# Three separate PSUM tiles for SwiGLU's seven products, a third plain block, and four early steps of the second product

## The chip, the core and the metric

The kernel runs on one core of a Trainium2 chip. The metric is the time of one launch on the device, in microseconds (us). Each kernel was run several times; its median is quoted, and one further execution was recorded by the hardware profiler, which is where all rows below come from.

## The reference, cut to what matters

One decoder layer with 1024 tokens of width 1024, all in float32. A token mixer with three branches comes first. The part that the change touches is the second half, SwiGLU with 2816 hidden columns:

```
x = layer_norm(ALPHA * x + (1 + g1) * mixer(...), ln1_g, ln1_b)
u = x * (1 + sc2) + sh2
gate, up = split(u @ ffn_w1, 2)           # (1024x1024) @ (1024x5632)
h = (silu(gate) * up) @ ffn_w2            # (1024x2816) @ (2816x1024)
x = layer_norm(ALPHA * x + (1 + g2) * h, ln2_g, ln2_b)
```

## The kernel before, in words

**Precision.** Every float32 operand is split into two parts, a rounded "high" part and the remainder ("low"). ScalarE (ACT) makes the high part and VectorE (DVE) the low one (`split`, lines 106 to 108). A product is three matmuls: high by high, high by low, low by high. A matmul has 128 weights rows and columns and 512 moving columns and writes 128x512 floats of PSUM, which are one of the two halves of a 128x1024 tile.

**First product.** The 2816 hidden columns are 22 blocks of 128. The first `NPL` blocks are "plain": gate and up are computed by `dense` (line 143) for all 1024 tokens, 2 parts x 8 slices of the contraction x 3 x 2 halves of the tokens = 96 matmuls. The other blocks use a Strassen-Winograd scheme over the four quarters (halves of the contraction by gate and up): seven products (`product`, line 1103) of 4 x 3 = 12 matmuls each, 84 in all, from sums of weights (`sums`: s1, s2, s3, s4 and the plain quarters, made one block ahead) and from sums of activations T1 to T4 (lines 1154 to 1168, made once, into buffers that the plain blocks read too).

In a block the seven products are issued in this order: py with s2 and T2; px with w11; pz with s1 and T1; py with s3 and T3, added to the first; px with w12, added; pz with s4, added; py with w22 and T4, added. Between them ACT copies py and px out (`u2_`, L1176, and `p1`, L1179), DVE adds pz to `p1` (`q_`, L1183) and then py to `q_` (L1186), ACT applies silu to px (L1191). So the sum of pz has to be read before the sixth product may write pz again, and the sum of py before the seventh. `banks` (the lines quoted here) gives the three places:

```
xy = pso.tile([P, T], F32, name="pxy", tag=f"o{i % 3}")
return xy[:, 0:HF], xy[:, HF:T], pso.tile([P, HF], F32, name="pz", tag="t", bufs=2)
```

px and py are the halves of one tile; the tiles o0, o1, o2 are taken in turn. The pools of PSUM here are declared with `reuse_waits="tile"`, and the layer that records the program puts the waits in from the tiles that instructions read and write.

**What sets the order.** Engines run their instructions in the order of the built program. A scheduler sets it from the order of the code, from priorities and from when buffers come free; matmuls of a product are tied behind those of the product before (`issue_after`). The weights of the blocks are loaded by SyncE (SP) into two buffers (`wraw`) and two more (`gate`), a load being issued when the buffer's last reader is done; the split weights stand in two buffers as well (`wh`, `wl`).

**Second product.** 22 steps of 128 hidden rows, for each half of the tokens; a step is 4 tiles of tokens x 3 x 2 halves = 24 matmuls (line 1219). The first `AHEAD` steps take their operands in buffers of the first product (`wraw`, `wh`, `wl`, `gate` and the s buffers). After them the buffers of the first product are given back, and `operands` fills new ones (`w2raw`, `hraw`, `w2h`, `w2l`, `hh`, `hl`) that lie in the same memory. At that place rows of the layer norm are loaded as well; DVE scales two of them (l1g, L1246, and l1b, L1247), and then GpSimd (POOL) multiplies and adds them to four tiles x1r, two instructions of 128x1024 each (L1270, L1271).

Of the kernel before, what the change touches and what calls it, by code (L numbers as in the profile page):

```python
# [9 lines left out]
F32 = mybir.dt.float32  # L10
F32R = mybir.dt.float32r
# [6 lines left out]
P = 128  # L18
D = 1024
T = 1024  # L20
KT = D // P
NTT = T // P
HF = 512
# [20 lines left out]
def trunk(ctx: ExitStack, tc: tile.TileContext, a: dict, out: bass.AP, scratch: dict):  # L44
# [10 lines left out]
    x = a["x"].rearrange("o t d -> (o t) d")  # L55
    y = out.rearrange("o t d -> (o t) d")
# [49 lines left out]
    def split(raw, hi, lo_):  # L106
        S.activation(hi, raw, AF.Copy)  # L107
        V.tensor_tensor(lo_, raw, hi.bitcast(F32), OP.subtract)  # L108
# [61 lines left out]
    def half(h):  # L170
        return slice(h * HF, (h + 1) * HF)
# [838 lines left out]
    pso = ctx.enter_context(tc.tile_pool(name="pso", bufs=1, space=PSUM, reuse_waits="tile"))  # L1010
    with tc.tile_pool(name="wo", bufs=2, reuse_waits="tile") as wo:
# [4 lines left out]
        for t in range(NTT):  # L1016
# [21 lines left out]
            for g, pt in enumerate(pts):  # L1038
                for j in range(4):
                    k = 4 * g + j  # L1040
                    PE.transpose(pt[:, j, :], t1[:, k * P:(k + 1) * P], ident)
                ut = par[1].tile([P, 4, P], F32, name="ut", tag="ord", bufs=4)
                for j in range(4):
                    k = 4 * g + j
# [9 lines left out]
    B12, B22 = [(u2h[k][1], u2l[k][1]) for k in range(4)], [(u2h[k][1], u2l[k][1]) for k in range(4, KT)]  # L1054
    f1_ctx = ExitStack()
    f1 = f1_ctx.enter_context(tc.tile_pool(name="f1", bufs=1, reuse_waits="tile"))
    NPL = 2

    def banks(i):
        xy = pso.tile([P, T], F32, name="pxy", tag=f"o{i % 3}")  # L1060
        return xy[:, 0:HF], xy[:, HF:T], pso.tile([P, HF], F32, name="pz", tag="t", bufs=2)


    for i in range(NPL):
        plain = []
# [41 lines left out]
    def loads(i):  # L1107
        raw = []
        for part, (pool, tag) in enumerate(((wpool, "wraw"), (gpool, "gate"))):
            c0 = part * HID + i * P  # L1110
            raw.append(pool.tile([P, KT, P], F32, name="w1raw", tag=tag))
            nc.sync.dma_start(raw[part], w1[:, c0:c0 + P].rearrange("(k p) c -> p k c", p=P))
        return raw

    def sums(raw):

        w = {}

        def parts_of(name, x):
            w[name] = [f1.tile([P, 4, P], F32R, name=f"s{name}{m}", bufs=2 if name == 22 else 1)  # L1120
                       for m in "hl"]
            split(x, *w[name])

        a11, a12, a21, a22 = (r[:, 4 * q:4 * q + 4] for r in raw for q in range(2))
        s1, s2, s3, s4 = (tmp().rearrange("p (k c) -> p k c", k=4) for _ in range(4))
        V.tensor_tensor(s1, a21, a22, OP.add)
        V.tensor_tensor(s2, s1, a11, OP.subtract)
        yield w
        parts_of(2, s2)
        V.tensor_tensor(s3, a11, a21, OP.subtract)  # L1130
        V.tensor_tensor(s4, a12, s2, OP.subtract)
        yield w
        wh = wpool.tile([P, KT, P], F32R, name="wh", tag="wh")
        wl = wpool.tile([P, KT, P], F32R, name="wl", tag="wl")
        split(raw[0], wh, wl)
        w[11], w[12] = ([m[:, 4 * q:4 * q + 4] for m in (wh, wl)] for q in range(2))
        yield w
        parts_of(22, a22)
        yield w
        parts_of(1, s1)  # L1140
        parts_of(3, s3)
        yield w
        parts_of(4, s4)
        yield w
# [3 lines left out]

    raws = {NPL: loads(NPL), NPL + 1: loads(NPL + 1)}
    gen = sums(raws.pop(NPL))  # L1150
    for _ in range(6):
# [17 lines left out]

    for i in range(NPL, NHB):  # L1170
        gen = sums(raws.pop(i + 1)) if i + 1 < NHB else None
        px, py_, pz = banks(i)
        p1, u2_, q_ = [f1.tile([P, HF], F32, name="c", bufs=5) for _ in range(3)]
        sg = [f1.tile([P, HF], F32, name="ht", bufs=3) for _ in range(2)]
# [30 lines left out]
    def accumulators():  # L1205
        acc = []
        for t in range(4):
            if t < 3:
                both = pso.tile([P, T], F32, name="accf", tag=f"o{(t + 1) % 3}")
                acc.append([both[:, half(h)] for h in range(2)])  # L1210
            else:
                acc.append([pso.tile([P, HF], F32, name="accf", tag="t", bufs=2) for _ in range(2)])
        return acc

    def step(acc, k, t, ops, halves=(0, 1)):
        wh, wl, hh, hl = ops
        for m_, w_ in ((hh, wh), (hh, wl), (hl, wh)):
            for h in halves:
                mm(acc[t][h], m_[:, t * P:(t + 1) * P], w_[:, half(h)],  # L1219
                   start=(k == 0 and m_ is hh and w_ is wh), stop=(k == NHB - 1 and m_ is hl))  # L1220


    acc = accumulators()
    AHEAD = 2
    for k in range(AHEAD):
        raw = wpool.tile([P, D], F32, name="w2raw", tag="wraw")
        nc.sync.dma_start(raw, w2[k * P:(k + 1) * P, :])
        wh, wl = (wpool.tile([P, D], F32R, name="w2" + m, tag="w" + m) for m in "hl")
        split(raw, wh, wl)
        raw = gpool.tile([P, HF], F32, name="hraw", tag="gate")  # L1230
        nc.scalar.dma_start(raw, scratch["h"][k * P:(k + 1) * P, half(0)])
        hh, hl = (f1.tile([P, HF], F32R, name=f"s{2 - k}{m}") for m in "hl")
        split(raw, hh, hl)
        with tc.issue_after(last[-1]):
            for t in range(4):
                step(acc, k, t, (wh, wl, hh, hl))
# [3 lines left out]
    with tc.tile_pool(name="f2", bufs=2, reuse_waits="tile") as f2, \  # L1240
# [7 lines left out]
        for grp in range(2):  # L1248
# [4 lines left out]
            def operands(k, pool):  # L1253
                raw = f2a.tile([P, D], F32, name="w2raw", bufs=2)
                nc.sync.dma_start(raw, w2[k * P:(k + 1) * P, :])
                wh = pool.tile([P, D], F32R, name="w2h")
                wl = pool.tile([P, D], F32R, name="w2l")
                split(raw, wh, wl)
                raw = f2a.tile([P, HF], F32, name="hraw", bufs=2)
                nc.scalar.dma_start(raw, scratch["h"][k * P:(k + 1) * P, hs])  # L1260
                hh = pool.tile([P, HF], F32R, name="hh")
                hl = pool.tile([P, HF], F32R, name="hl")
                split(raw, hh, hl)
                return wh, wl, hh, hl
# [8 lines left out]
            late = LATE[grp]  # L1273
            for k in range(0 if grp else AHEAD, NHB - late):
                ops = operands(k, f2a)
# [50 lines left out]
```

## Time and profile before

| what | value |
|---|---|
| median of three runs | 2179.4 us (2179.03 to 2179.47) |
| the profiled execution, whole | 2177.67 us |
| its span, first to last instruction | 2175.9 us |
| mean granted TensorE clock, share of full | 0.972 |
| TensorE busy | 2046.6 us, 94% |
| VectorE, ScalarE, GpSimd busy | 1262.0, 766.8 and 212.7 us |

The profiled execution took 1.73 us less than the median, and 1.77 us more than its span. The times in rows count from the start of the span. A matmul's row starts at its issue; rows of back-to-back matmuls overlap, so the time that a matmul costs is read from the distance of starts and not from its duration. A name in square brackets at the end of a row is what ended the idle time before it.

### The profile page before, as it was taken

To read this page: it belongs to the slowest core of one execution; us is meant where nothing else is said; L and a number is where in the kernel's file an instruction comes from. 1 tells how busy PE (TensorE), PEld (TensorE's weight loads), DVE (VectorE), ACT (ScalarE), POOL (GpSimd) and SP (SyncE) were. 2 spreads that over 40 slices of the span, in tenths; PEclk is the share of its full clock that TensorE was granted. 3 is DMA by queue.
4 is the path that set the end of the run, shared out by engine and by line. 5 is a ranking of instruction groups with operands and counts; after the bars stand their busy time and mean duration, and the time that the engine had idled before them with its cause. 6 is when DMAs were issued, how large, how long until landed. Compare 5 with 4: busy or idle time off the path is not lost.

```text
span 2175.9 us, 26614 instructions
## 1 busy us (share of the span) xinstructions
PE 2046.6 (94%) x10242; PEld 1595.4 (73%) x10242; DVE 1262.0 (58%) x2324; ACT 766.8 (35%) x1236; POOL 212.7 (10%) x251
## 2 busy tenths in 40 slices
PE   6999999999999999999999999997999999989997
PEld 4777777776777777777767887876777777768776
DVE  6585555735735666455674576577555555354755
ACT  3524323234134343444444234542323232223242
POOL 1101002001010000011121000000000000040703
PEclk9999989979999999999999999999999999989999
DMA  9111111211113453211104654222222222265361
GB/s 281 49 59 44 45 49 35 63 40 39 59 46 107 142 151 99 59 37 37 37 28 156 213 158 159 89 78 78 62 83 69 77 73 68 74 216 171 132 194 69
DMA packets 190095, 202.71 MB, mean 93 GB/s; under 512 B 9852, under 2 KB 145168, under 8 KB 189968
## 3 DMA queue, kind: packets, MB, share of 16 engines
q1 hardware_dynamic: 159216, 133.22, 20.6%
q10 hardware_dynamic: 29920, 66.70, 8.9%
q8 instruction: 81, 1.33, 0.2%
q0 software_dynamic: 832, 1.09, 0.2%
q14 instruction: 46, 0.38, 0.1%
HBM read 162.16 MB, written 38.81 MB: 92 GB/s over the span
## 4 chain that ended last, share of the span: by engine, by line
PE 73%; DVE 12%; issue 6%; ACT 5%; DMA 3%; POOL 1%; SPq 1%; ACTq 0%; DVEq 0%; POOLq 0%
PE psd L143 20%; PE pxy L1103 13%; PE accf L1219 9%; PE pj L143 6%; PE pz L1103 5%; PE woa L1024 3%; PE po L865 2%; PE pt L851 2%; DVE tw L473 1%; DVE TI L475 1%; PE pm L458 1%; PE pss L835 1%; PE pw L525 1%; PE pst L537 1%; DVE VS L705 1%
## 5 line engine op out<-in xcount | busy, mean ns | idle before, releaser
L143 PE MATMUL psd<-ul,wh 128*128 128x512 f32 x992 | 337.8, 411 | 1.9 <-DVE ul L274 1.8
L143 PE MATMUL psd<-uh,wh 128*128 128x512 f32 x992 | 334.0, 409 | 0.7 <-ACT uh L272 0.5
L143 PE MATMUL psd<-uh,wl 128*128 128x512 f32 x992 | 332.4, 408 | 1.1 <-DVE wl L120 1.1
L143 PEld LDWEIGHTS psd<-ul,wh 128*128 128x128 f32 x992 | 184.1, 191 | 45.0 <-issue 9.4
L143 PEld LDWEIGHTS psd<-uh,wh 128*128 128x128 f32 x992 | 185.5, 191 | 41.6 <-issue 6.8
L143 PEld LDWEIGHTS psd<-uh,wl 128*128 128x128 f32 x992 | 185.0, 191 | 40.6 <-issue 6.5
L107 ACT ACTIVATE wh<-wraw 128x1024 fp32r<-128x1024 f32 (+1 forms) x87 | 81.8, 940 | 325.9 <-PE psd L143 254.0
L108 DVE TENSOR_TENSOR wl<-wraw,wh 128x1024 fp32r<-128x1024 f32 (+1 forms) x87 | 93.1, 1071 | 58.1 <-ACT wh L107 55.8
L1219 PE MATMUL accf<-w2h,hh 128*128 128x512 f32 x336 | 112.6, 397 | 13.8 <-ACT w2h L107 9.1
L1219 PE MATMUL accf<-w2l,hh 128*128 128x512 f32 x336 | 112.8, 398 | 3.7 <-DVE w2l L108 3.7
L1219 PE MATMUL accf<-w2h,hl 128*128 128x512 f32 x336 | 111.9, 395 | 0.0
L1103 PE MATMUL pxy<-oh,wh 128*128 128x512 f32 x160 | 68.0, 425 | 44.0 <-DVE c L1186 24.2
L1270 POOL TENSOR_TENSOR x1r<-x1r,l1g 128x1024 f32<-128x1024 f32 x8 | 21.3, 2672 | 841.1 <-DVE l1g L1246 753.4
L108 DVE TENSOR_TENSOR w2l<-w2raw,w2h 128x1024 fp32r<-128x1024 f32 x44 | 63.6, 1445 | 44.8 <-ACT w2h L107 44.8
L1219 PEld LDWEIGHTS accf<-w2h,hh 128*128 128x128 f32 x336 | 64.3, 192 | 28.4 <-ACT w2h L107 10.0
L1103 PEld LDWEIGHTS pxy<-oh,wh 128*128 128x128 f32 x160 | 30.5, 191 | 66.3 <-DVE c L1186 32.7
L1219 PEld LDWEIGHTS accf<-w2l,hh 128*128 128x128 f32 x336 | 64.3, 192 | 18.3 <-DVE w2l L108 4.9
L1219 PEld LDWEIGHTS accf<-w2h,hl 128*128 128x128 f32 x336 | 64.7, 193 | 13.8
L108 DVE TENSOR_TENSOR hl<-hraw,hh 128x512 fp32r<-128x512 f32 x42 | 43.3, 1036 | 46.5 <-ACT hh L107 46.5
L843 POOL TENSOR_SCALAR sc<-sc,mx 128x128 f32<-128x128 f32 (+7 forms) x64 | 49.0, 769 | 217.9 <-DVE mx L842 181.7
L107 ACT ACTIVATE w2h<-w2raw 128x1024 fp32r<-128x1024 f32 x44 | 46.2, 1052 | 52.8 <-DMA w2raw<-in_ffn_w_dram 27.5
L841 ACT ACTIVATE sc<-sc,mx 128x128 f32<-128x128 f32 (+7 forms) x64 | 49.6, 775 | 42.4 <-DVE mx L840 36.5
(442 smaller groups left out, 4286.2 us busy)
## 6 DMA issues: line engine op xcount, KB each, us to landing
wraw<-in_w_in_dram SPq DMA_DIRECT2D x62, 512.0 KB, 4.0
w2raw<-in_ffn_w_dram SPq DMA_DIRECT2D x44, 512.0 KB, 3.8
w1raw<-in_ffn_w_dram SPq DMA_DIRECT2D x40, 512.0 KB, 4.0
wada<-in_w_ada_dram SPq DMA_DIRECT2D x64, 256.0 KB, 2.9
s_gate<-gate ACTq DMA_DIRECT2D x24, 512.0 KB, 2.9
gate<-s_gate ACTq DMA_DIRECT2D x24, 512.0 KB, 4.2
s_h<-ht ACTq DMA_DIRECT2D x44, 256.0 KB, 2.2
hraw<-s_h ACTq DMA_DIRECT2D x44, 256.0 KB, 2.9
```

Of the source, the lines that this page charges most:

```text
L107: S.activation(hi, raw, AF.Copy)
L108: V.tensor_tensor(lo_, raw, hi.bitcast(F32), OP.subtract)
L143: i = mm(ps[:, h * HF:(h + 1) * HF], w[:, k, :], u[k][h], start=(k == 0 and w is wh and u is uh), stop=(k == nk - 1 and w is wl))
L458: mm(pm[hd][:, :, j], BK[hr, c].rearrange("p a b -> p (a b)"), AR[hr, c], start=True, stop=True)
L473: V.tensor_tensor(t3, X[:, s + 1:32, s:s + 1].to_broadcast([64, ni, nj]), TI[:, s:s + 1, 0:nj].to_broadcast([64, ni, nj]), OP.mult)
L841: S.activation(sc[:, 0:n], sc[:, 0:n], AF.Exp, bias=mx[:, 2:3], accum_out=mx[:, 3:4])
L843: G.tensor_scalar(sc[:, 0:n], sc[:, 0:n], mx[:, 4:5], 1.0, op0=OP.mult, op1=OP.mult)
L851: PE.transpose(pt[:, j, :], sc[:, (k0 + j) * P:(k0 + j + 1) * P], ident)
L865: mm(po[hr, q0:2 * P], VT[:, kj, hr], PTs[hd][:, kj, q0:2 * P], start=(kj == 0), stop=(kj == nk - 1))
L1024: mm(acc[:, half(h)], m_[k][h2][:, tl], w_[h], start=(k == 0 and m_ is mh and w_ is wh), stop=(k == KT - 1 and m_ is ml))
L1103: ins = mm(ps, w[i][:, k, :], u[k][j], start=(start and k == 0 and m == 0), stop=(stop and k == 3 and m == 2), skip_group_check=not start)
L1219: mm(acc[t][h], m_[:, t * P:(t + 1) * P], w_[:, half(h)], start=(k == 0 and m_ is hh and w_ is wh), stop=(k == NHB - 1 and m_ is hl))
```

## The change

```
     NPL = 3                                   # was 2
     def banks(i):
-        xy = pso.tile([P, T], F32, name="pxy", tag=f"o{i % 3}")
-        return xy[:, 0:HF], xy[:, HF:T], pso.tile([P, HF], F32, name="pz", tag="t", bufs=2)
+
+        px, py_ = (pso.tile([P, T], F32, name=f"p{n}", tag=f"o{t}") for n, t in (("x", 0), ("y", 1 + i % 2)))
+        return px[:, 0:HF], py_[:, 0:HF], pso.tile([P, HF], F32, name="pz", tag="t", bufs=2)
...
-    AHEAD = 2
+    AHEAD = 4
...
-        hh, hl = (f1.tile([P, HF], F32R, name=f"s{2 - k}{m}") for m in "hl")
+        hh, hl = (f1.tile([P, HF], F32R, name=f"s{(2, 1, 3, 4)[k]}{m}") for m in "hl")
```

px is now always tile o0, py o1 or o2 in turn, and pz is as it was; half of o0, o1 and o2 stays unused. Block 2 is plain, so 19 blocks use the seven products instead of 20. Steps 2 and 3 of the second product take their operands in the first product's buffers too; their h rows go to the buffers s3 and s4. Line numbers behind `banks` are one higher in the changed kernel.

On TensorE, in a block in the middle of the first product, this is the end of the fourth product and the start of the fifth, before (pxy is the tile of px and py, oh and ol the parts of the activations, wh and wl of the weights):

```order
L1103 MATMUL pxy<-uh_119,s3h 128x512
L1103 MATMUL pxy<-ul_135,s3h 128x512
L1103 MATMUL pxy<-uh_119,s3l 128x512
L1103 MATMUL pxy<-oh_9139,wh 128x512 [waits DVE_49]
L1103 MATMUL pxy<-ol_9141,wh 128x512
L1103 MATMUL pxy<-oh_9139,wl 128x512
```

And now, first the same place, then the end of the fifth product and the start of the sixth:

```order
L1104 MATMUL py<-uh_119,s3h 128x512
L1104 MATMUL py<-ul_135,s3h 128x512
L1104 MATMUL py<-uh_119,s3l 128x512
L1104 MATMUL px<-oh_9139,wh 128x512 [waits Activation_49]
L1104 MATMUL px<-ol_9141,wh 128x512
L1104 MATMUL px<-oh_9139,wl 128x512
```

```order
L1104 MATMUL px<-oh_9144,wh 128x512
L1104 MATMUL px<-ol_9146,wh 128x512
L1104 MATMUL px<-oh_9144,wl 128x512
L1104 MATMUL pz<-uh_112,s4h 128x512 [waits DVE_49]
L1104 MATMUL pz<-ul_128,s4h 128x512
L1104 MATMUL pz<-uh_112,s4l 128x512
```

Before, the fifth product waits for DVE's read of py (L1186), which the fourth has just written; now it waits for ACT's copy of px, which the second wrote, and the wait for DVE stands at the sixth, for the read of pz that the third wrote.

On DVE, at the seam between the plain blocks and the first block of seven products, before (L1127, L1130 and L1131 make s2, s3 and s4 from w1raw, the weights of that block; wl is the low part of a plain block's weights):

```order
L108 TENSOR_TENSOR wl<-wraw,wh 128x1024
L1127 TENSOR_TENSOR s<-s,w1raw 128x512
L1077 TENSOR_TENSOR ht<-ht,pgu 128x512 x2
L108 TENSOR_TENSOR wl<-wraw,wh 128x1024
L108 TENSOR_TENSOR s2l<-s,s2h 128x512
L1130 TENSOR_TENSOR s<-w1raw 128x512
L1131 TENSOR_TENSOR s<-w1raw,s 128x512
```

And now:

```order
L108 TENSOR_TENSOR wl<-wraw,wh 128x1024
L1078 TENSOR_TENSOR ht<-ht,pgu 128x512 x2
L108 TENSOR_TENSOR wl<-wraw,wh 128x1024 x2
L1128 TENSOR_TENSOR s<-s,w1raw 128x512
L1131 TENSOR_TENSOR s<-w1raw 128x512
L1132 TENSOR_TENSOR s<-w1raw,s 128x512
L108 TENSOR_TENSOR s2l<-s,s2h 128x512
```

The low part of the third plain block's first weights (the second of the "x2") stands ahead of the sums now, and the load of their w1raw goes into the buffer that it frees.

On DVE, at the seam between the two products, before (hl is the low part of a step's h rows, w2l of its weights; the l1g and l1b rows are those that POOL waits for):

```order
L1201 TENSOR_TENSOR ht<-ht,c 128x512
L1246 TENSOR_SCALAR l1g<-l1g 128x1024
L1247 TENSOR_SCALAR l1b<-l1b 128x1024
L108 TENSOR_TENSOR hl<-hraw,hh 128x512
L108 TENSOR_TENSOR w2l<-w2raw,w2h 128x1024
```

And now:

```order
L1202 TENSOR_TENSOR ht<-ht,c 128x512
L108 TENSOR_TENSOR w2l<-w2raw,w2h 128x1024
L1247 TENSOR_SCALAR l1g<-l1g 128x1024
L1248 TENSOR_SCALAR l1b<-l1b 128x1024
L108 TENSOR_TENSOR w2l<-w2raw,w2h 128x1024
L108 TENSOR_TENSOR hl<-hraw,hh 128x512
L108 TENSOR_TENSOR w2l<-w2raw,w2h 128x1024
```

The w2l of step 2 stands ahead of l1g and l1b, that of step 3 behind them; the hl and w2l after those are step 4's, the first with new buffers.

## Rows read from the trace of the kernel before

**Rows 1.** The page: the span, a group of ACT's instructions, loads of w1.
```profile
span 2175.9 us, 26614 instructions
L107 ACT ACTIVATE w2h<-w2raw 128x1024 fp32r<-128x1024 f32 x44 | 46.2, 1052 | 52.8 <-DMA w2raw<-in_ffn_w_dram 27.5
w1raw<-in_ffn_w_dram SPq DMA_DIRECT2D x40, 512.0 KB, 4.0
```

**Rows 2.** Stretches: length, busy PE, PEld, DVE, ACT, POOL; clock; DMA share, GB/s.
```profile
1357.00:1377.00 20.00, 20.00 (x98) 16.75 (x97) 10.41 (x30) 11.53 (x35) 0.00 (x0) 1.00 0.21 81
1453.93:1492.64 38.71, 25.23 (x85) 18.68 (x85) 36.85 (x59) 13.52 (x21) 0.00 (x0) 0.78 0.18 54
1492.64:1899.53 406.89, 373.04 (x1598) 296.62 (x1596) 213.48 (x308) 120.06 (x187) 0.00 (x0) 1.00 0.23 71
1899.53:1929.91 30.38, 19.51 (x73) 15.13 (x72) 15.72 (x9) 3.78 (x5) 16.24 (x6) 0.78 0.67 237
```

**Rows 3.** TensorE's waits, 1490 to 1900 us: total, times, longest.
```profile
PE pxy L1103 <- ACT c L1176: 19.0, 19, 1.0
PE pxy L1103 <- DVE c L1186: 14.8, 19, 0.8
```

**Rows 4.** Timeline, TensorE, one block of seven products: start, duration, instruction.
```profile
1557.00 0.39 PE L1103 MATMUL pxy<-uh,s2h 128*128 128x512 f32 x1
...
1560.92 0.50 PE L1103 MATMUL pxy<-oh,wh 128*128 128x512 f32 x1 [1.04 <-ACT c L1176]
...
1570.16 0.50 PE L1103 MATMUL pxy<-oh,wh 128*128 128x512 f32 x1 [0.78 <-DVE c L1186]
...
1578.45 0.39 PE L1103 MATMUL pxy<-uh,s2h 128*128 128x512 f32 x1
```

**Rows 5.** Timeline, TensorE: second plain block, first block of seven products.
```profile
1432.17 0.39 PE L143 MATMUL pgu<-oh,wh 128*128 128x512 f32 x1
...
1453.71 0.39 PE L143 MATMUL pgu<-uh,wl 128*128 128x512 f32 x1
...
1456.91 0.76 PE L1103 MATMUL pxy<-uh,s2h 128*128 128x512 f32 x1 [2.81 <-DVE ht L1077]
...
1482.17 0.79 PE L1103 MATMUL pxy<-oh,wh 128*128 128x512 f32 x1 [9.42 <-DVE c L1186]
...
1487.19 0.39 PE L1103 MATMUL pz<-uh,s4h 128*128 128x512 f32 x1
```

**Rows 6.** Timeline, DVE, the same seam.
```profile
1433.10 0.69 DVE L1127 TENSOR_TENSOR s<-s,w1raw 128x512 f32<-128x512 f32 x1 [4.08 <-DMA w1raw<-in_ffn_w_dram]
...
1479.11 0.68 DVE L1131 TENSOR_TENSOR s<-w1raw,s 128x512 f32<-128x512 f32 x1
1479.71 0.68 DVE L1183 TENSOR_TENSOR c<-c,pz 128x512 f32<-128x512 f32 x1
```

**Rows 7.** Timeline, TensorE, the first step with new buffers.
```profile
1918.47 1.22 PE L1219 MATMUL accf<-w2h,hh 128*128 128x512 f32 x2 [7.91 <-ACT w2h L107]
1922.66 1.22 PE L1219 MATMUL accf<-w2l,hh 128*128 128x512 f32 x2 [2.96 <-DVE w2l L108]
```

**Rows 8.** Timeline, ACT and its queue of DMAs, that seam.
```profile
1910.65 0.82 ACTq L1260 DMA_DIRECT2D hraw<-s_h  x2
1916.85 0.63 ACT L107 ACTIVATE hh<-hraw 128x512 fp32r<-128x512 f32 x1 [18.48 <-DMA hraw<-s_h]
```

**Rows 9.** Timeline, DVE, that seam.
```profile
1912.74 0.69 DVE L1246 TENSOR_SCALAR l1g<-l1g 128x1024 f32<-128x1024 f32 x1 [11.60 <-DMA l1g<-in_ln_g_dram]
1915.31 1.25 DVE L1247 TENSOR_SCALAR l1b<-l1b 128x1024 f32<-128x1024 f32 x1 [1.88 <-DMA l1b<-in_ln_b_dram]
...
1919.24 3.37 DVE L108 TENSOR_TENSOR w2l<-w2raw,w2h 128x1024 fp32r<-128x1024 f32 x1
1922.53 2.85 DVE L108 TENSOR_TENSOR hl<-hraw,hh 128x512 fp32r<-128x512 f32 x1
...
1937.57 1.21 DVE L108 TENSOR_TENSOR w2l<-w2raw,w2h 128x1024 fp32r<-128x1024 f32 x1
```

**Rows 10.** Timeline, POOL, that seam (x2: two instructions in turn).
```profile
1913.67 5.10 POOL L1270 TENSOR_TENSOR x1r<-x1r,l1g 128x1024 f32<-128x1024 f32 x2 [753.44 <-DVE l1g L1246]
```

More of the change, by code (lines that the diff above doesn't have):

```diff
@@ L1056, in trunk @@
     f1 = f1_ctx.enter_context(tc.tile_pool(name="f1", bufs=1, reuse_waits="tile"))
-    NPL = 2
+    NPL = 3
     def banks(i):
-        xy = pso.tile([P, T], F32, name="pxy", tag=f"o{i % 3}")
-        return xy[:, 0:HF], xy[:, HF:T], pso.tile([P, HF], F32, name="pz", tag="t", bufs=2)
+        px, py_ = (pso.tile([P, T], F32, name=f"p{n}", tag=f"o{t}") for n, t in (("x", 0), ("y", 1 + i % 2)))
+        return px[:, 0:HF], py_[:, 0:HF], pso.tile([P, HF], F32, name="pz", tag="t", bufs=2)
     for i in range(NPL):
```

## The prediction

> **What bounds the kernel now.** I read the page first, then the first product in windows, then TensorE's waits by releaser, then single blocks in the timeline, and last the two seams on every engine. TensorE is busy for nearly the whole span, so each microsecond in which it stands still is a microsecond of the result, and other engines matter only where it waits for them.
>
> Inside the plain blocks there is nothing to win: in a stretch of 20 us TensorE is busy for 20.00 at full clock [rows 2]. From the first matmul of the second plain block to its last there are 95 distances in 21.54 us, 0.2267 us each [rows 5]. At that pitch a plain block (96 matmuls) costs 21.76 us, a block of seven products (84) 19.04, one product (12) 2.72, one step of the second product (24) 5.44.
>
> A block of seven products really takes 21.42: the 19 undisturbed ones fill 406.89 us [rows 2]. The 2.38 us above 19.04 sit at two places: once per block TensorE waits for ACT's copy of py, and once for DVE's read of py, 19 times each, 19.0 and 14.8 us in all [rows 3]. In the timeline of one block they are 1.04 and 0.78 us, at the first matmul of the second and of the fifth product [rows 4]; the visible gaps make 1.78 a block, and the refilling of the pipeline behind them the other 0.6. Both releasers have the name of py and the waiting matmul writes px. They are waits for the neighbouring half of the same tile, not for data.
>
> Two seams are left. Between plain blocks and the others the first block of seven products takes 38.71 us at a granted clock of 0.78, with DVE busy for 36.85 of them [rows 2]: DVE makes the sums T1 to T4 while TensorE waits 2.81 and 9.42 us for it [rows 5]. Between the two products the first three steps take 30.38 us instead of 16.32, a loss of 14.06, at 0.78 again [rows 2]. Of it 10.87 are two waits at the third step, the first with new buffers [rows 7].
>
> **The blocks in the middle.** With px, py and pz in tiles of their own, a product waits for the last reader of its own tile alone. The second product (px) then waits for the silu of the block before, which can follow that block's fifth product at 5 x 2.72 = 13.6 us, say at 15.3, and is needed at 19.04 + 2.72 = 21.8 (6.5 to spare); the fifth (px) for ACT's copy of the second, two products old, the sixth (pz) for DVE's read of the third, the seventh (py) for DVE's read of the fourth. The third ends 8.2 us into a block; DVE is busy about half of the time (213.48 of 406.89 [rows 2]) with instructions of 0.60 us pitch [rows 6], so I put that read at about 9 us, against a need at 5 x 2.72 = 13.6: slack 4.7. The seventh has as much. DVE is therefore the cover, and it is not thin. I count 18 blocks (4 to 21) x (21.42 - 19.04) = **-42.7**. The least is half of it, if a wait of the size of the present second one (0.78 and its refill, about 1.1) stays in every block: -23.
>
> **The seam between plain blocks and the rest.** Before, block 2 (seven products) took 38.71 and block 3 an ordinary 21.42, together 60.13. Now block 2 is plain, 21.76, from 1453.93 to 1475.7. Its cover hides DVE's sums in part only. The chain: the third plain block's first weights may be split when the second block's first part has been read, half of the way between 1432.17 and 1453.71 [rows 5], at 1443.1; ACT takes 1.06 (nearest row: w2h 1052 ns [rows 1]), DVE 1.2, so 1445.3. The load of block 3's w1raw goes into the buffer that this frees and takes 4.1 (before, the same wait was 4.08 [rows 6], median 4.0 [rows 1]): 1449.4. Behind it on DVE stands L1128, and behind that the whole chain of sums up to the read of pz, L1184. That chain lasted 46.6 us, from 1433.10 to 1479.71, almost without a pause [rows 6]; 73 instructions of 0.60 and two wl of 1.2 now make 46.2. The read is over at about 1496. TensorE would be at the sixth product at 1475.7 + 13.6 = 1489.3. It waits 6.5 us, and then runs at half of the clock for a product: before, the 12 matmuls after the 9.42 us wait took 5.02 us instead of 2.72 [rows 5], 2.3 more. Block 3 costs 19.04 + 8.8 = 27.8; with the plain block 49.6 against 60.1: **-10.5**. Without a stall it would be -19.3. If the chain is 5 us later still (T3's last part is due at the fourth product with no slack by the same count), it is -5.
>
> That DVE is idle for about 13 us before the load lands is why a whole plain block does not buy the whole 21.8 us.
>
> **The seam between the products.** Count from the first matmul of the second product, 1899.53. Before, hraw of the third step was issued at +11.1, when step 1 was over, and hh started at +17.3 [rows 8]; w2h released TensorE at +18.9, w2l, slow on DVE, let it wait 2.96 more [rows 7]. Now four steps run from old buffers, until +21.8 at best. The fifth step's hraw is issued after step 2, at +16.3, so hh at +22.5 and w2h at +24: late by 2.3, where before it was late by 7.9.
>
> But a new wait comes in front of it. Step 3's w2l stands on DVE behind l1g and l1b, which wait for their loads; l1b ran at +15.8 to +17.0 [rows 9]. Two more steps' loads are in front of it now (0.5 MB each, the stretch moves 237 GB/s [rows 2], 2.2 us for one): w2l of step 3 is ready at +18 to +20, and needed at +16.8. So 1 to 3 us of wait at step 3 and up to 2.3 of half clock. And POOL's eight instructions, 2.55 us each [rows 10], start with l1g, at about +14, and last until +35: the hl and w2l of step 4 fall into them. There w2l took 3.37 us, and alone 1.21 [rows 9]; hl took 2.85.
>
> Bounds: with only w2h and w2l of step 4 late (2.3 and 2.3) the loss is 4.6, a gain of 9.5. With w2l of step 3 late by 3, its half clock 2.3, then hl, w2l of step 4 (3.37 + 2.85 behind w2h at +24, and half clock again), it is as before, about 14: gain 0. The rows nearest to the second case are of this very place, so I take a loss of 11, **-3**. It could be +4, if both half-clock stretches grow.
>
> By the Trainium skill's page "SBUF — State Buffer", section "Who interferes with whom", a DVE instruction with two SBUF inputs contends with a GpSimd instruction that reads SBUF, and the later of the two is blocked until the other is done. Rows 9 and 10 agree in direction: 3.37 against 1.21 is 2.16 more, and a POOL instruction lasts 2.55. By the rule each of step 4's two DVE instructions would wait up to a full 2.55, 3.8 and 3.2 us in all, 0.8 more than the rows, and the sum 2124.
>
> **The sum.** -42.7 - 10.5 - 3 = -56.2. The profiled execution took 2177.67, so 2121.5; the median stands 1.73 above it: **2123 us**. What follows the third step took 246 us (2175.9 - 1929.91 [rows 1, 2]); I take it as unchanged, the fourth and fifth step, which stood at its start, at 5.44 each as before.
>
> **Rivals.**
> - A: the seams go well, no chain is late (gain 9.5 at the second, up to 4 more at the first): 2113. For it: the wait by w2h falls to 2.3 by count. Against: DVE's chains at both seams. 17%.
> - B: the blocks gain, but the seams give nothing or small waits stay in every block (up to 1.1 x 18 = 20): 2128 to 2146. For it: DVE is the releaser at every place I named. 21%.
> - C: the change does not do what it says; the waits in the blocks come back under another releaser (px has one tile now instead of three in turn, so silu or the copy p1 holds it): only the seams gain, 2123 + 42.7 = 2166. Against: 6.5 us to spare. 3%.
> - D, the other side: loads of w1 set the pace. L1128 stands on DVE ahead of the read of pz and waits for a load that, by the order of the code, is issued about 2 us into a block and lands at 6. The blocks shorten by 11%, so DMA's share of 0.23 [rows 2] becomes 0.26. The slack is 4.7 us; a load of over 8.8 us eats it. At the second seam 0.25 MB took 6.2 us, from 1910.65 to 1916.85 [rows 8], an estimate of 12.4 for 0.5 MB; the blocks would lose 3.6 x 18 = 65 and the kernel ends at 2188. Against: that was at a share of 0.67, and w1's loads take 4.0 [rows 1]. 3%.
> - The forecast: 56%.
>
> **Range and chances.** The forecast's own bounds are about 2117 to 2130. With A and the nearer part of B the range is 2110 to 2138. A measurement of this kernel can tell about 0.2%, 4.4 us. Only D, and a sum of mishaps that no row supports, is above 2183.8: slower 0.03, within 0.2% 0.02, faster 0.95.
>
> **What would show it.** In the middle blocks no wait of L1104 by u2_'s ACT copy or L1187, 18 blocks in about 343 us at clock 1.00, and the first product over at about 1847 instead of 1899.5. At the first seam one wait of 6 to 7 us for DVE's L1184 at the sixth product of the first block, with half clock behind it. At the second, a wait for w2l at the fourth step, a short one for w2h at the fifth, and 38 us for the first five steps instead of 27.2. The prediction is wrong if the blocks stay over 20 us, if the wait at the first seam is gone or over 12 us, or if the second loses over 16.

## The result, and the profile after

The changed kernel takes 2124.6 us, median of four runs (2121.4 to 2127.8), against 2179.4 (2179.03 to 2183.67): a ratio of 0.9744, 95% interval 0.9723 to 0.9765. The prediction said 2123, 2110 to 2138. The profiled execution has a span of 2120.7 us, 55.2 less than before.

In stretches (columns as in [rows 2]: length, busy time of PE, PEld, DVE, ACT and POOL, granted clock, DMA share, GB/s), the first product from its third plain block on and the second product:

```profile
1452.58:1474.34 21.76, 21.76 (x97) 18.02 (x96) 21.69 (x36) 7.75 (x12) 0.00 (x0) 1.00 0.23 73
1474.34:1502.17 27.83, 21.66 (x86) 17.35 (x85) 27.65 (x45) 11.35 (x19) 0.00 (x0) 0.88 0.18 58
1502.17:1844.88 342.71, 342.71 (x1513) 283.88 (x1512) 203.23 (x298) 114.96 (x179) 0.00 (x0) 1.00 0.27 83
1844.88:1887.48 42.60, 32.36 (x121) 25.41 (x120) 19.24 (x13) 7.49 (x9) 21.46 (x8) 0.84 0.56 198
1887.48:2120.70 233.22, 215.60 (x937) 177.02 (x935) 128.88 (x150) 73.93 (x98) 63.96 (x36) 0.97 0.46 149
```

The third line is the main effect: TensorE is busy for 342.71 of 342.71 us, 19.04 a block, where 19 blocks filled 406.89 with 373.04 busy [rows 2]. Stage by stage:

| stage | before | after | difference | predicted |
|---|---|---|---|---|
| up to the second plain block's first matmul | 1432.17 | 1430.82 | -1.35 | 0 |
| second plain block | 21.76 | 21.76 | 0 | 0 |
| blocks 2 and 3 | 38.71 + 21.42 | 21.76 + 27.83 | -10.54 | -10.5 |
| blocks 4 to 21 | 385.47 | 342.71 | -42.76 | -42.7 |
| second product, steps 0 to 4 | 41.28 | 42.60 | +1.32 | -3 |
| all behind them | 235.09 | 233.22 | -1.87 | 0 |
| span | 2175.9 | 2120.7 | -55.2 | -56.2 |

The stretches of the kernel before for the rows on blocks 4 to 21, on steps 0 to 4 and on all behind them:

```profile
1514.06:1899.53 385.47, 353.44 (x1514) 281.00 (x1512) 201.74 (x291) 113.64 (x177) 0.00 (x0) 1.00 0.23 71
1899.53:1940.81 41.28, 30.41 (x122) 24.16 (x121) 23.70 (x13) 7.88 (x10) 23.43 (x8) 0.83 0.62 215
1940.81:2175.90 235.09, 216.71 (x937) 177.82 (x935) 130.07 (x151) 74.48 (x100) 64.00 (x36) 0.96 0.46 150
```

TensorE's waits from 1440 to 1890 us of the changed kernel (in total, times, longest):

```profile
PE accf L1220 <- DVE w2l L108: 9.0, 2, 5.2
PE pz L1104 <- DVE c L1184: 6.2, 1, 6.2
PE accf L1220 <- ACT w2h L107: 1.3, 1, 1.3
```

The 19 waits for u2_'s copy and the 19 for DVE's read of py [rows 3] are gone, and no other name has taken their place. The second line is the predicted stall of the first block of seven products. In the timeline (start, duration, instruction), where before the fifth product started after 9.42 us [rows 5]:

```profile
1494.27 0.80 PE L1104 MATMUL pz<-uh,s4h 128*128 128x512 f32 x1 [6.17 <-DVE c L1184]
...
1499.43 0.40 PE L1104 MATMUL py<-uh,s22h 128*128 128x512 f32 x1
```

The twelve matmuls of the sixth product take 5.16 us instead of 2.72; the clock granted from 1494.27 to 1499.43 is 0.52 of full. DVE, same place:

```profile
1442.59 1.23 DVE L108 TENSOR_TENSOR wl<-wraw,wh 128x1024 fp32r<-128x1024 f32 x1 [9.08 <-ACT wh L107]
1447.67 0.69 DVE L1128 TENSOR_TENSOR s<-s,w1raw 128x512 f32<-128x512 f32 x1 [3.85 <-DMA w1raw<-in_ffn_w_dram]
...
1493.54 0.68 DVE L1184 TENSOR_TENSOR c<-c,pz 128x512 f32<-128x512 f32 x1
```

Between the second and the third line are 45.87 us of instructions without a pause; in front of the first two DVE stood for 9.08 and 3.85 us.

At the seam of the products, TensorE, then DVE, then POOL (to hold against [rows 7], [rows 9] and [rows 10]; the second product starts at 1844.88):

```profile
1867.03 1.22 PE L1220 MATMUL accf<-w2l,s4h 128*128 128x512 f32 x2 [5.21 <-DVE w2l L108]
...
1875.58 0.73 PE L1220 MATMUL accf<-w2h,hh 128*128 128x512 f32 x2 [1.26 <-ACT w2h L107]
1880.08 1.22 PE L1220 MATMUL accf<-w2l,hh 128*128 128x512 f32 x2 [3.77 <-DVE w2l L108]
```

```profile
1859.86 0.69 DVE L1247 TENSOR_SCALAR l1g<-l1g 128x1024 f32<-128x1024 f32 x1 [7.02 <-DMA l1g<-in_ln_g_dram]
1862.41 1.29 DVE L1248 TENSOR_SCALAR l1b<-l1b 128x1024 f32<-128x1024 f32 x1 [1.85 <-DMA l1b<-in_ln_b_dram]
1863.62 3.35 DVE L108 TENSOR_TENSOR w2l<-w2raw,w2h 128x1024 fp32r<-128x1024 f32 x1
1874.62 2.12 DVE L108 TENSOR_TENSOR hl<-hraw,hh 128x512 fp32r<-128x512 f32 x1 [7.64 <-ACT hh L107]
1876.66 3.37 DVE L108 TENSOR_TENSOR w2l<-w2raw,w2h 128x1024 fp32r<-128x1024 f32 x1
```

```profile
1860.79 5.10 POOL L1271 TENSOR_TENSOR x1r<-x1r,l1g 128x1024 f32<-128x1024 f32 x2 [701.22 <-DVE l1g L1247]
```

The 7.9 us wait for w2h has shrunk to 1.26, and a wait of 5.21 has come in front of it: step 3's w2l stands behind l1g and l1b, and takes 3.35 with POOL at work from 1860.79 (what each of the two costs is tried below).

### The profile page after: what moved, and what is told of

Same layout as the page of the kernel before. It is cut to its first block, busy times and chain, and to the rows that moved or that the text cites. A ratio compares the mean times of both kernels' runs of the same rounds, so it can differ in the third digit from the quotient of the medians.

```text
span 2120.7 us, 26608 instructions
## 1 busy us (share of the span) xinstructions
PE 2035.2 (96%) x10254; PEld 1601.4 (76%) x10254; DVE 1246.7 (59%) x2311; ACT 763.2 (36%) x1230; POOL 210.2 (10%) x251
## 4 chain that ended last, share of the span: by engine, by line
PE 75%; DVE 11%; issue 6%; ACT 4%; DMA 3%; POOL 1%; SPq 1%; DVEq 0%; POOLq 0%; ACTq 0%
PE psd L143 21%; PE accf L1220 9%; PE py L1104 7%; PE pj L143 6%; PE pz L1104 5%; PE px L1104 5%; PE woa L1024 3%; PE po L865 2%; PE pt L851 2%; PE pgu L143 2%; DVE tw L473 1%; DVE TI L475 1%; PE pm L458 1%; PE pss L835 1%; PE pw L525 1%
## 5 line engine op out<-in xcount | busy, mean ns | idle before, releaser
L1220 PE MATMUL accf<-w2h,hh 128*128 128x512 f32 x320 | 107.1, 395 | 6.3 <-DVE t1f L1289 4.6
L1220 PE MATMUL accf<-w2l,hh 128*128 128x512 f32 x320 | 107.0, 396 | 4.7 <-DVE w2l L108 4.7
L1220 PE MATMUL accf<-w2h,hl 128*128 128x512 f32 x320 | 106.8, 395 | 0.0
L108 DVE TENSOR_TENSOR hl<-hraw,hh 128x512 fp32r<-128x512 f32 x40 | 37.9, 952 | 51.7 <-ACT hh L107 51.6
L529 ACT ACTIVATE UV<-pu 64x64 f32<-64x64 f32 x64 | 13.7, 214 | 140.5 <-PE pu L528 139.9
L107 ACT ACTIVATE w2h<-w2raw 128x1024 fp32r<-128x1024 f32 x44 | 46.2, 1052 | 48.8 <-DMA w2raw<-in_ffn_w_dram 27.6
L143 PE MATMUL pj<-ol,wh 128*128 128x512 f32 x192 | 59.4, 390 | 0.0
```

What stands on the lines that cost most here:

```text
L143: i = mm(ps[:, h * HF:(h + 1) * HF], w[:, k, :], u[k][h], start=(k == 0 and w is wh and u is uh), stop=(k == nk - 1 and w is wl))
L1220: mm(acc[t][h], m_[:, t * P:(t + 1) * P], w_[:, half(h)], start=(k == 0 and m_ is hh and w_ is wh), stop=(k == NHB - 1 and m_ is hl))
```

## The experiments

### Each part of the change alone

The first is `banks` of the change alone; the second `NPL = 3`; the third `AHEAD = 4` with its buffers s3 and s4; the fourth the change with `AHEAD = 2`.

> The three tiles alone; two plain blocks and two early steps as before. Theory (the waits in the blocks are waits for the other half of one tile): blocks 3 to 21 fall from 21.42 to 19.04 us each, 19 x 2.38 = 45.2; in block 2 the wait moves from the fifth product to the sixth, where DVE's read of pz ends at about 1480.4, so that block takes some 34 us instead of 38.7, 4.5 less. Sum -49.7: 2129.7 us. Rival (the tiles gain only together with the third plain block, since DVE is too late for the sixth product in every block): blocks stay over 20.5 us and the kernel over 2155.

Measured: 2129.2 us, ratio 0.977 (0.9747 to 0.9793). Block 2, then blocks 3 to 21, and the wait:

```profile
1459.90:1493.18 33.28, 24.20 (x86) 18.68 (x85) 32.82 (x54) 12.92 (x22) 0.00 (x0) 0.85 0.15 48
1493.18:1854.94 361.76, 361.76 (x1598) 299.55 (x1597) 213.95 (x314) 120.11 (x187) 0.00 (x0) 1.00 0.26 81
```

```profile
1486.00 0.79 PE L1104 MATMUL pz<-uh,s4h 128*128 128x512 f32 x1 [4.68 <-DVE c L1184]
```

361.76 / 19 = 19.04: the three tiles alone take away every wait in the blocks, with two plain blocks as before. Block 2 falls by 5.4, expected were 4.5; it holds one more long wait, 4.05 us for ACT's uh, where the kernel before waited 2.81 for ht [rows 5].

> The third plain block alone, with px and py in one tile and two early steps. Theory: blocks 4 to 21 stay at 21.42 us; the first block of seven products waits at its fifth product for DVE's read of py at the end of the same chain of sums, 12 to 13 us, and takes about 35; with the plain block 56.7 us against 60.1, so -3.4: 2176 us. Rival (the plain block covers DVE's sums, and its gain has nothing to do with the tiles): the stall is gone, -17 to -19: 2161.

Measured: 2172.1 us, 0.9975 (0.996 to 0.999). Block 3, blocks 4 to 21, and the wait:

```profile
1475.76:1507.13 31.37, 21.03 (x85) 16.67 (x84) 30.85 (x50) 11.75 (x18) 0.00 (x0) 0.84 0.19 61
1507.13:1892.49 385.36, 353.33 (x1514) 281.04 (x1513) 201.81 (x291) 113.60 (x177) 0.00 (x0) 1.00 0.23 71
```

```profile
1497.44 0.79 PE L1103 MATMUL pxy<-oh,wh 128*128 128x512 f32 x1 [9.66 <-DVE c L1186]
```

385.36 / 18 = 21.41, unchanged. The stall stays, 9.66 us instead of 9.42: the chain of sums begins 16.0 us later (1449.10 against 1433.10 [rows 6]), and TensorE comes to the fifth product 15.0 later. Block 3 took 31.4, not 35, as the expected wait of 12 to 13 us was too long. The plain block gains 7.0 here (60.13 - 21.76 - 31.37); the rival is out. Beside separate tiles it gains less: with the tiles alone blocks 2 and 3 take 33.28 + 19.04 = 52.32, in the changed kernel 49.59, so 7.8 of that seam's 10.5 come with the tiles and 2.7 with the plain block.

> Four early steps alone. As predicted: -3, 2176.4 us. By the trace of the changed kernel, where the five first steps took 42.60 us against 41.28 and what follows 1.87 less: -0.5, 2178.9 us, with a wait of about 5 us for w2l at the fourth step and about 5 us in two waits at the fifth. Rival (four steps gain here, and the changed kernel lost it to a first product that is faster): the five steps take 38 us and the time is 2175 or less.

Measured: 2176.8 us, 0.9999 (0.9987 to 1.0012). Its waits at the seam:

```profile
1920.26 1.22 PE L1219 MATMUL accf<-w2l,s4h 128*128 128x512 f32 x2 [5.59 <-DVE w2l L108]
1929.21 0.73 PE L1219 MATMUL accf<-w2h,hh 128*128 128x512 f32 x2 [1.26 <-ACT w2h L107]
1933.34 1.22 PE L1219 MATMUL accf<-w2l,hh 128*128 128x512 f32 x2 [3.40 <-DVE w2l L108]
```

> The change without its third part: three tiles, three plain blocks, two early steps. As predicted, the four steps are worth 3, so 2127.6 us here. By the trace of the changed kernel they are worth nothing, 2125 us, and the third step waits for w2h and w2l as in the kernel before. Rival (the four steps cost): 2121 or less.

Measured: 2123.7 us, 0.9751 (0.9728 to 0.9773). Its waits there:

```profile
1866.15 1.22 PE L1220 MATMUL accf<-w2h,hh 128*128 128x512 f32 x2 [8.19 <-ACT w2h L107]
1869.92 1.22 PE L1220 MATMUL accf<-w2l,hh 128*128 128x512 f32 x2 [2.55 <-DVE w2l L108]
```

The four steps are worth nothing that can be measured, in either kernel. Executions of one kernel scatter by several us (23 of the kernel before, run beside these, took 2171.4 to 2185.6), and some of it lies ahead of the first product, where the code is the same (its first matmul came at 1407.96 us in the changed kernel's profile and at 1415.28 in that of the tiles alone). So the second product is better told by the stretch from its first matmul to the end of the span:

| kernel | first matmul | span | stretch |
|---|---|---|---|
| before | 1899.53 | 2175.9 | 276.37 |
| four steps alone | 1897.74 | 2174.6 | 276.86 |
| changed kernel without them | 1846.92 | 2122.8 | 275.88 |
| changed kernel | 1844.88 | 2120.7 | 275.82 |

### The first seam: the sums of u ahead of the weights

```
     raws = {NPL: loads(NPL), NPL + 1: loads(NPL + 1)}
-    gen = sums(raws.pop(NPL))
-    for _ in range(6):
-        w = next(gen)
     t1f, t2f = [], []
...
+    gen = sums(raws.pop(NPL))
+    for _ in range(6):
+        w = next(gen)
+
     for i in range(NPL, NHB):
```

> The changed kernel with T1 to T4 written ahead of the first block's weight sums, so that DVE makes them in the time in which it waited for the load of w1raw. Theory (the 6.2 us wait at the sixth product of the first block is DVE's chain started late by that load, and the half clock follows from the wait): the wait is gone, that block takes 19.04 us instead of 27.83: -8.8, 2115.8 us. Rival (T4, which overwrites operands that the last plain block still reads, keeps the chain late wherever the load is): a wait of over 4 us stays at the sixth or seventh product, 2120 or more.

Measured: 2117.2 us, 0.9718 (0.9691 to 0.9745). Second and third plain block, then block 3:

```profile
1433.02:1454.78 21.76, 21.76 (x97) 18.02 (x96) 21.76 (x35) 8.13 (x13) 0.00 (x0) 1.00 0.23 73
1454.78:1476.54 21.76, 21.76 (x97) 18.02 (x96) 21.58 (x35) 8.51 (x14) 0.00 (x0) 1.00 0.40 121
1476.54:1495.58 19.04, 19.04 (x85) 15.77 (x84) 11.83 (x17) 6.66 (x10) 0.00 (x0) 1.00 0.26 84
```

The second plain block in the changed kernel:

```profile
1430.82:1452.58 21.76, 21.76 (x97) 18.02 (x96) 8.55 (x12) 5.11 (x8) 0.00 (x0) 1.00 0.31 97
```

Block 3 costs 19.04, 8.79 less, and no wait of TensorE is left in the first product, so the rival (T4) is out. DVE is busy for all of the second plain block, where in the changed kernel it was for 8.55 us of 21.76. The stall was made by the order on DVE: instructions that needed no load stood behind one that waited for it.

### The second seam: the order on DVE, and POOL

First l1g and l1b are only tied behind the low part of step 3's weights:

```
-        split(raw, wh, wl)
+        low = split(raw, wh, wl)          # split returns its DVE instruction
...
-        V.tensor_scalar(ag, ag, ALPHA, None, op0=OP.mult)
-        V.tensor_scalar(ab, ab, ALPHA, None, op0=OP.mult)
+        with tc.issue_after(low):
+            V.tensor_scalar(ag, ag, ALPHA, None, op0=OP.mult)
+            V.tensor_scalar(ab, ab, ALPHA, None, op0=OP.mult)
```

> The changed kernel with l1g and l1b tied on DVE behind the low part of step 3's weights; POOL's work starts as soon as they are done, about 2 us later than now. Theory (step 3 waited for its w2l because DVE stood at l1g and l1b, whose loads land late): the 5.2 us wait and its half clock are gone, step 4 keeps its two waits of 1.3 and 3.8: -7.5, 2117 us. Rival (w2l of step 3 is late by its own weights): the wait stays over 3 us, 2121 or more.

Measured: 2114.9 us, 0.9704 (0.9682 to 0.9725). The second product's stretch is 2117.4 - 1848.75 = 268.65, 7.2 less. Step 3's wait is gone; the first waits are step 4's:

```profile
1871.93 0.73 PE L1220 MATMUL accf<-w2h,hh 128*128 128x512 f32 x2 [1.26 <-ACT w2h L107]
1875.94 1.22 PE L1220 MATMUL accf<-w2l,hh 128*128 128x512 f32 x2 [3.27 <-DVE w2l L108]
```

Then l1g, l1b and the eight POOL instructions stand behind step 9's operands:

```
+            def rows_x1():
+                if not grp:
+                    with tc.issue_after(low[-1]):
+                        V.tensor_scalar(ag, ag, ALPHA, None, op0=OP.mult)
...
+                if k == 10 and not grp:
+                    rows_x1()
                 ops = operands(k, f2a)
```

> The changed kernel with l1g, l1b and POOL's eight instructions tied behind step 9's operands. Theory (step 4's 3.8 us wait is DVE slowed by POOL): besides the wait at step 3 that one goes too, w2l takes 1.2 us there, and the five first steps take 30 to 32 us instead of 42.6: -11, 2113.5 us. Rival (POOL has nothing to do with step 4's wait): same as with the order alone, 2117. Second rival (POOL's work takes the time later, in steps 10 to 14): waits for w2l of some 3 us there, 2116.

Measured: 2115.5 us, 0.9706 (0.9684 to 0.9727); by the median no better than the order alone. The stretch tells them apart: 2113.3 - 1848.75 = 264.55, 4.1 less than there and 11.3 less than in the changed kernel. One trace of each stands behind that. The wait for w2l has fallen to 0.53:

```profile
1871.94 0.73 PE L1220 MATMUL accf<-w2h,hh 128*128 128x512 f32 x2 [1.26 <-ACT w2h L107]
1873.20 0.73 PE L1220 MATMUL accf<-w2l,hh 128*128 128x512 f32 x2 [0.53 <-DVE w2l L108]
```

DVE at step 4, and later while POOL works:

```profile
1870.97 0.69 DVE L108 TENSOR_TENSOR hl<-hraw,hh 128x512 fp32r<-128x512 f32 x1 [8.76 <-ACT hh L107]
1871.92 1.23 DVE L108 TENSOR_TENSOR w2l<-w2raw,w2h 128x1024 fp32r<-128x1024 f32 x1 [0.25 <-ACT w2h L107]
...
1893.55 2.88 DVE L108 TENSOR_TENSOR hl<-hraw,hh 128x512 fp32r<-128x512 f32 x1
1896.35 3.43 DVE L108 TENSOR_TENSOR w2l<-w2raw,w2h 128x1024 fp32r<-128x1024 f32 x1
```

```profile
1887.35 8.53 POOL L1275 TENSOR_TENSOR x1r<-x1r,l1g 128x1024 f32<-128x1024 f32 x3 [723.32 <-DVE l1g L1270]
```

The same instructions take 0.69 and 1.23 without POOL, 2.88 and 3.43 beside it: 2.2 more each, at either length, as long as both engines work without a pause (the first to meet POOL gets less, as hl with 2.12 in the changed kernel). POOL is held up in turn: its instruction takes 2.38 where DVE is idle (1871.48 in the changed kernel), 2.84 on average here. TensorE does not wait for any of these from 1885 to 1930, since by then DVE is some steps ahead; the second rival is out. By the Trainium skill's page "SBUF — State Buffer", section "Who interferes with whom", the later of a DVE instruction with two SBUF inputs and a GpSimd instruction that reads SBUF is blocked until the earlier is done; the trace agrees in that the 2.2 us do not depend on the DVE instruction's own length and are close to the 2.38 of one POOL instruction.

Both seams mended:

> The changed kernel with T1 to T4 first and with the rows and POOL's work behind step 9. Theory (two separate seams): the sum of the two, -8.8 - 11 = -19.8: 2104.8 us. Rival (what is won at a seam is lost behind it): over 2110.

Measured: 2103.9 us (2100.7 to 2107.3), 0.9651 (0.963 to 0.9672), which beats both kernels; nothing is given back behind the seams. Blocks 3, 4 to 21, and all from the second product's first matmul:

```profile
1476.82:1495.86 19.04, 19.04 (x85) 15.77 (x84) 11.78 (x17) 6.66 (x10) 0.00 (x0) 1.00 0.26 83
1495.86:1838.58 342.72, 342.72 (x1513) 283.78 (x1512) 200.14 (x293) 114.94 (x179) 0.00 (x0) 1.00 0.26 82
1838.58:2102.20 263.62, 244.20 (x1057) 200.00 (x1055) 154.45 (x162) 81.50 (x107) 87.08 (x44) 0.98 0.49 164
```

### What the other two parts are worth in that kernel

In it `AHEAD = 2`, and then, with four steps again, `NPL = 2`:

> The kernel with T1 to T4 first and the rows later, with two early steps instead of four. Theory (the four steps take away the 8 us wait for w2h, and in the changed kernel DVE's l1g, l1b and POOL took it back): without them that wait is there again, about 8 us and 2 of half clock: +9, 2113 us. Rival (the four steps are worth nothing in any case): 2104 to 2106.

Measured: 2114.0 us, 0.9721 (0.9699 to 0.9742), and 2112.2 - 1838.59 = 273.61 us for the second product, 10.0 more:

```profile
1857.95 1.22 PE L1221 MATMUL accf<-w2h,hh 128*128 128x512 f32 x2 [8.31 <-ACT w2h L107]
```

So the four steps are worth 10 us once DVE's queue and POOL are out of the way; in the changed kernel these two took all of it back.

> The same kernel with four early steps and two plain blocks. Theory (the third plain block is the cover under which DVE makes the sums): block 2 is 2.7 us shorter, but its s2l stands on DVE behind the second plain block's silu products and some 17 instructions of 0.6, so its first product waits about 10 us and runs on at half clock: 2112 to 2115. Rival (with the sums of u first two plain blocks are enough): 2101.

Measured: 2117.4 us, 0.9732 (0.9711 to 0.9753), over the 2112 to 2115 expected. Told by the stretch from the first product's first matmul to the second's, it is 1852.05 - 1413.18 = 438.87 us against 1838.58 - 1410.44 = 428.14 with three plain blocks, so 10.7 more; of the 13.2 by which the spans differ another 2.7 lie ahead of the first product:

```profile
1468.97 0.79 PE L1104 MATMUL py<-uh,s2h 128*128 128x512 f32 x1 [11.01 <-ACT s2h L107]
```

The wait is for s2h, which ACT makes from L1128's sum, and not for s2l as expected; that sum stands on DVE behind those of u and ends at 1468.26. The third plain block is needed as cover for the sums, also when they are in the better order.

### How much slack DVE has in a block

```
-        V.tensor_tensor(q_, p1, pz, OP.add)
+        for _ in range(4):                # in the other kernel 7
+            V.tensor_tensor(q_, p1, pz, OP.add)
```

> The changed kernel with DVE's sum of p1 and pz made four times in each block instead of once (the same result; the sixth product waits for the last). In the order of DVE three other instructions stand between them, so the last ends at about 4.1 us after the first; in the trace of the changed kernel the first ends 4.1 us ahead of the sixth product. Theory (DVE has a slack of about 4 us in a block): the blocks stay at 19.04 or grow by under 0.5 us, 2125 to 2134. Rival (the blocks run at the edge of DVE): over 1.5 us a block, 2152 or more.

> The same with seven sums instead of one. Theory: the last ends about 6 us after the first, 1.3 to 2 us late for the sixth product; with the refill each block takes 20.5 to 21.5 us, 18 x 2 = 36 more: 2150 to 2170. Rival (the slack is larger, the waits were only read so): under 2135.

Measured: 2132.3 and 2167.5 us, one run each. TensorE's waits in the middle blocks, the first from 1502, the second from 1510 to 1840:

```profile
PE pz L1104 <- DVE c L1185: 0.7, 2, 0.5
```

```profile
PE pz L1104 <- DVE c L1185: 24.0, 15, 2.6
```

With four sums the last starts 3.6 us after the first in the middle blocks (4.1 in the first block of seven products), and TensorE waits there twice, 0.7 us in all. The span is 9.9 us longer than the changed kernel's: 4.1 are the stall of the first block (10.3 instead of 6.2), 2.4 lie ahead of the first product, 1.9 behind it, and 1.5 are left for the blocks. With seven sums the last starts 5.8 us after the first, and there are 15 waits of 1.6 on average. The slack lies between; predicted were 4.7, and the trace of the changed kernel reads 4.1 in one block:

```profile
1606.23 0.68 DVE L1184 TENSOR_TENSOR c<-c,pz 128x512 f32<-128x512 f32 x1
```

with the sixth product's first matmul at 1610.96. Over the 18 blocks the same distance is 2.7 to 4.6.

## Why the prediction was right, point by point

- **The blocks in the middle.** Term -42.7, measured -42.76. Shown by the tiles alone: the waits were for the other half of a tile and go with it; what is late next (DVE's read of pz) comes 2.7 to 4.6 us early.
- **The first seam.** Term -10.5, measured -10.54. The chain was worked out from the right link: block 3's w1raw comes into the buffer that the third plain block's first weights free. That landed 1.7 us earlier than worked out (1447.67, and the run was 1.35 ahead), the chain lasted 45.9 instead of 46.2, the wait 6.17 instead of 6.5. That the order was the cause, and could be changed, the prediction did not say; it only noted DVE's idle time.
- **The second seam.** Term -3, measured +1.32 up to the fifth step and -0.55 with all behind it. This step failed. The wait for w2l of step 3 was placed rightly but sized at 1 to 3 us, with w2l at its undisturbed 1.2; it was 5.21. By the rows 2.1 of that are POOL's (3.35 instead of 1.23): POOL starts as soon as l1g is scaled, with only l1b between it and that w2l on DVE, and I had let its work fall on step 4 alone. The other 3.1 are the queue behind l1g and l1b. At step 4 the wait for w2h was sized at 2.3 and was 1.26; hl and w2l took 2.12 and 3.37 there, where the prediction had 2.85 and 3.37 by its rows and up to 3.2 and 3.8 by the rule that it cites. That this rule's sum, 2124, is the nearest to the 2124.6 measured is luck. The 1.87 us won behind the fifth step were not forecast: in a stretch of 40 us that begins 119 us later the granted clock was 0.96 before and is 1.00 now, and no run shows that the change did it. That the bound of no gain stood in the range was right; the choice inside it was 2.5 us off. The span fell by 1.0 less than the sum of 56.2: 2.5 by this term, less 1.35 ahead of the first product, where the code is the same; that the two partly cancel is luck as well.
- **The rivals.** A is out: the first seam kept its stall, and the second gave nothing. D (loads set the pace) is out: the blocks run at 19.04, and DVE's wait for w1raw in them (35.5 us in all from 1440 to 1850, 15 times, 3.3 at most) lies inside the slack. C is out. Of B the half on the seams came true for the second.

## What to carry to other kernels

A wait by a tile's other half looks like a data wait in a list of waits; compare the tile that the waiting instruction writes with the one the releaser reads. Before buying a late operand more time, read what stands in front of its producer on that engine: four early steps were worth nothing until two small instructions that waited for a load, and POOL's work that they release, were moved behind it, and 10 us after. The same holds for covers: beside the separate tiles the third plain block was worth 2.7 us, with the sums of u first 10.7.

## Not expected of the hardware

A short wait may or may not cost the clock. With seven sums a block, one wait of 1.78 us was followed by a stretch at a granted clock of 0.76, one of 2.63 us by one at full clock (each from the sixth product's first matmul to the next block's):

```profile
1590.65:1597.85 7.20, 7.20 (x24) 5.75 (x25) 3.67 (x5) 1.29 (x3) 0.00 (x0) 0.76 0.26 73
1614.25:1619.82 5.57, 5.57 (x24) 4.61 (x25) 3.66 (x5) 1.27 (x2) 0.00 (x0) 1.00 0.32 94
```

So the length of the last wait alone does not tell; what decides stays open here.
